# An encoder block on one core: the next head's convolution is issued inside the present head, the norms' products apart from their sums, and the first half's final norm between the second half's products

## The chip, the cores and the metric

The kernel runs on one core of a Trainium2 chip. A core has five engines with one instruction stream each: TensorE (PE, matrix products; its weight loads are listed as PEld and run beside the products), VectorE (DVE), ScalarE (ACT), GpSimd (POOL, hardly used here) and SyncE (SP), whose stream issues the DMA transfers. Each engine works through its own stream in order, and semaphores hold an instruction until what it reads is there and what it writes over has been read. The metric is device time in microseconds (us): median of three runs.

## What is computed

The reference, cut to what matters (D_MODEL = SEQ = 1024, hidden width 2816, four LRU heads of 256 channels):

```
u = rms_norm(x, g_mix);  u_a, x_b, gate_b, merge_a, merge_b = split(u @ w_in)
g_a      = gelu(u_a * s5_d + S5(u_a, forward) + S5(u_a, backward))
branch_a = (g_a * sigmoid(g_a @ s5_glu_w + s5_glu_b)) @ w_a_out
xc  = depthwise_conv4(x_b) + bias                       # RG-LRU, head by head
per direction d: r, i = sigmoid(xc @ wa + ba), sigmoid(xc @ wx + bx)
                 a = exp(-8 r softplus(-a_logit))
                 h_b += linear_scan(a, sqrt(1 - a*a) * (i * xc), reverse = d)
branch_b = (h_b * gelu(gate_b)) @ w_b_out
h = x + (sigmoid(merge_a)*branch_a + sigmoid(merge_b)*branch_b) @ w_o
v = rms_norm(h, g_ffn)
h = h + (silu(v @ w_ff_gate) * (v @ w_ff_up)) @ w_ff_down
h = h + sigmoid(rms_norm(h, g_ple) @ w_ple_gate) * (p @ w_ple_proj)
return rms_norm(h, g_final)
```

## The kernel before, in words

Activations lie feature by feature: a tile holds 128 features on the partitions and 1024 positions (or a half of 512). Every fp32 operand of a product is split into a high part and a rest (names that end in `h` and `l`); `gemm` forms three products per block of 128 by 128: high by high, rest by high, high by rest. A 128x512 product is one matmul, so a block of 1024 features against one tile of outputs is 24 products per half.

The order of work is that of the code, changed by a scheduler that builds each engine's stream. `hp()` raises a piece's priority; a tile waits for a free buffer of its pool. The pools that matter here: `l`, 16 tiles of 1024 for the LRU (`lslot`); `o`, 3 staging tiles (`ot`); two PSUM buffers `pg` for the gate products; from the Wo stage on, 8 PSUM banks.

The stages by the time at which they lie in the profiled execution: 0 to 505 us first norm, the projections u, x, g and the S5 branch; 505 to 698 the last projections (`pi_b`, `pi_a`), among whose products the LRU heads stand; 698 to 820 the S5 gate (`pgl`); 820 to 936 the product with w_a_out (`pao`); 936 to 1030 that with w_b_out (`pbo`); 1030 to 1136 w_o, half by half (`pwo`, with `pxr`, the transposes of x); 1136 to 1187 the first products of five hidden tiles (`head_group`: `q1`, `q2`) and the embedding's projection (`embed_proj`: `ppj`); 1187 to 1586 the hidden groups (`hidden_group`: up to seven products `q1` to `q7` of half size each); 1586 to 1835 the down projection (`pfd`), whose last block goes half by half; 1835 to the end the embedding's gate (`ppg`), half by half, and after each half the final norm (`pq`, sums; `pfin`, transposes back).

An LRU head (`lru_head`) begins with its convolution (`lru_conv`: per feature tile one ACT Identity at L718, three DVE operations at L719 to L721, the cast `xch` at L723 and the rest `xcl` at L724). Then per direction four gate products `pg` (24 products each on the operands `xch`, `xcl`; sigmoid to `tg`, tanh to `ls`) and the chain on DVE and ACT to the scan (L755 to L776). The heads are a generator of 16 steps, which `lru_step(share)` moves on between projections: `lru_step((i + 1) / NF)` after the i-th.

A norm (`rstd_parts`) sums squares (`pss`, products of one column, L942), works out the reciprocal root on DVE and ACT into a diagonal `dg`, and spreads it over the partitions by a product `psr` (L952). For the first half of w_o and both halves of the down projection the two products are issued one after the other (`rstd_half`).

A hidden group loads two weight tiles (L1045: `fg` for the gate, `fu` for up, into an `o` buffer) and makes sums and differences of them (`s1` to `s4`), the operands of `q3` to `q7`. A head group's result goes to DRAM as `hdd`, an `embed_proj` result as `prd`, both from `o` buffers.

Of the kernel before, what the change touches and what calls it, by code (L numbers as in the profile page):

```python
# [8 lines left out]
F32 = mybir.dt.float32  # L9
# [14 lines left out]
FILL = (1, 1, 1, 2)  # L24
PORD = "xgba"
NL = 16
LRUT = 6
MI = 2
WS, WH = 2, 3
XB = 2  # L30
# [4 lines left out]
D = 1024  # L35
# [18 lines left out]
def block_kernel(tc, a, out):  # L54
# [653 lines left out]
    def lru_conv(hd):  # L708
# [18 lines left out]
            xcl.append(cl)  # L727
        return xc, xch, xcl

    def lru_head(hd):  # L730
        xc, xch, xcl = lru_conv(hd)
        hf = [None, None]
        for d in range(2):
            with hp():
                st = wstage([128, 2, 2, 256], "l")
                for q, nm in enumerate(("lru_wa", "lru_wx")):
                    dma(st[:, q], a[nm][0, d, hd].rearrange("(k p) n -> p k n", p=128))
                wh, wl = split(st, [128, 2, 2, 256], "l")
            cc = [d * 8 + 2 * hd + m for m in range(2)]
            tr, ti, s, z = [], [], [], []  # L740
            for m in range(2):
                for bn, dst, q in (("lru_ba", tr, 0), ("lru_bx", ti, 1)):
                    ps = psb("pg")
                    gemm(ps, (wh[:, q], wl[:, q]), xch, xcl, ms=slice(m * 128, (m + 1) * 128))
                    t = lslot("tg")
                    A.activation(t, ps, AF.Sigmoid, bias=vcol(bn, cc[m]))
                    dst.append(t)

                s.append(lslot("ls"))
                A.activation(s[m], tr[m], AF.Tanh, scale=sp4[:, cc[m]:cc[m] + 1])  # L750
                V.tensor_tensor(ti[m], ti[m], xc[m], MUL)
                if m == 0:
                    yield
            for m in range(2):
                A.activation(tr[m], tr[m], AF.Exp, scale=spm8[:, cc[m]:cc[m] + 1])  # L755
                A.activation(tr[m], tr[m], AF.Identity, bias=ones[:, 0:1])

                z.append(lslot("lz"))
                V.scalar_tensor_tensor(z[m], s[m], 1.0, tr[m], ADD, MUL)
                V.scalar_tensor_tensor(z[m], z[m], 4.0, tr[m], SUB, MUL)  # L760
                V.tensor_scalar(tr[m], z[m], -0.5, -1.0, MUL, ADD)
                V.scalar_tensor_tensor(ti[m], z[m], -1.0, ti[m], MUL, MUL)
            for m in range(2):
                A.activation(s[m], s[m], AF.Sqrt, scale=0.25)
            for m in range(2):
                V.tensor_tensor(ti[m], ti[m], s[m], MUL)
                f = 2 * hd + m
                if d == 0:
                    V.tensor_tensor_scan(z[m], tr[m], ti[m], 0.0, MUL, ADD)
                    hf[m] = z[m]  # L770
                else:
                    V.tensor_tensor_scan(z[m][:, ::-1], tr[m][:, ::-1], ti[m][:, ::-1], 0.0, MUL, ADD)  # L772
                    V.tensor_tensor(hf[m], hf[m], z[m], ADD)
                    gg = lslot("gg")
                    dma(gg, ggd[f])
                    V.tensor_tensor(gg.rearrange("p (j c) -> p j c", j=8), hf[m].rearrange("p (c j) -> p j c", j=8),  # L776
                                    gg.rearrange("p (j c) -> p j c", j=8), MUL)
                    dma(ybd[f], gg)
            yield
# [52 lines left out]

    left = list(left)
    gp = []
    NF = len(left) + 8 + LRUT
    for i, kf in enumerate(left):
        inproj(*kf)
        if len(left) - i <= 4:
            gp.append(load_split(gd, len(gp), "ga", 1.0, y2))
        lru_step((i + 1) / NF)  # L840


    yad = [dram(f"yad{f}", [128, 1024]) for f in range(8)]
# [4 lines left out]
    for m in range(8):  # L848
        w = wload(a["s5_glu_w"][0][:, m * 128:(m + 1) * 128], f"gl{m}")
        ps = psm("pgl")  # L850
        gemm(ps, w, [x[0] for x in gp], [x[1] for x in gp])
        with hp():
            t = ot("glt")
            A.activation(t, ps, AF.Sigmoid, bias=vcol("s5_glu_b", m))
            g = ot("glg")
            dma(g, gd[m])
            V.tensor_tensor(t, t, g, MUL)
            dma(yad[m], t)
        if 1 <= m <= 4:
            yp.append(load_split(yad, m - 1, "ya", 1.0, r1))  # L860
        lru_step((len(left) + m + 1) / NF)
    while len(yp) < 8:
        yp.append(load_split(yad, len(yp), "ya", 1.0, y2))
    bp = []
    for m in range(8):
        w = wload(a["w_a_out"][0][:, m * 128:(m + 1) * 128], f"ao{m}")
        ps = psm("pao")
        gemm(ps, w, [x[0] for x in yp], [x[1] for x in yp])
        with hp():
            t = ot("ta")  # L870
            dma(t, mad[m])
            V.tensor_tensor(t, t, ps, MUL)
            dma(brd[m], t)
        lru_step((len(left) + 8 + m + 1) / NF)
        if m >= 4:
            bp.append(load_split(ybd, m - 4, "yb", 1.0, r1))
    while len(bp) < 8:
# [60 lines left out]
    def rstd_parts(n, acc):  # L938
# [13 lines left out]
        T.matmul(ps, ones, dg, start=True, stop=True)  # L952
        A.copy(rstd[:, half(n)], ps)
        yield

    def rstd_half(n, acc):
        for _ in rstd_parts(n, acc):
            pass

    def sumsq(h, first, acc):  # L960
        if first:
# [145 lines left out]
    def hidden_group(ht):  # L1107
# [3 lines left out]
        with hp(HPW):  # L1111
            w1 = raw_w(wg[:, cs], f"fg{ht}", "ws")
            w2 = raw_w(wu[:, cs], f"fu{ht}", "o")
            o = group_ops(w1, w2, f"_{ht}", head)
            ru = r1("ru", F32)
            if head:
                dma(ru, hdd[ht])
        p1, c11 = ru[:, 0:512], ru[:, 512:1024]
        if not head:
            q1 = bank("q1")  # L1120
# [61 lines left out]
    for n in range(2):  # L1182
        acc = qp.tile([128, 512], F32, name="acc", tag="acc", bufs=2)
        for m in range(8):
# [12 lines left out]
            V.tensor_tensor(h, h, ps, ADD)  # L1197
            dma(hsd[m][:, half(n)], h)
            sumsq(h, m == 0, acc)
            if n == 1 and m in (3, 5):  # L1200
                embed((m - 3) // 2)
            if n == 1 and m < 4:
                operands_first(m)
        if n == 0:
            rstd_half(n, acc)

# [15 lines left out]
    next(bcast)  # L1224
    fill(it, 0)
    fill(embed_proj(0), 0)
    next(bcast)
    fill(embed_proj(1), 1)
    pp = iter(range(2, 8))
    for ht in range(1, NHEAD):  # L1230
        it = head_group(ht)
        next(it)
        fill(it, FH)
        for m in [next(pp, None) for _ in range(2)]:
            if m is not None:
                fill(embed_proj(m), FP)
    for it in late:
        next(it)
    for _ in rest:
        pass  # L1240
    for ht in range(NHID):
        hidden_group(ht)


    hres = [r1(f"h{m}", F32) for m in range(8)]
# [24 lines left out]
    for k in range(8):  # L1270
        t = r1(f"uh{k}")
        uh.append([t[:, half(n)] for n in range(2)])
        ul.append([None, None])
    accs = []
    for n in range(2):
        acc = qp.tile([128, 512], F32, name="acc", tag="acc", bufs=2)
        accs.append(acc)
        cs = slice(n * 512, n * 512 + 512)
        for m2 in range(4):
            w = wload(wd[(h0 - nb) * 128:h0 * 128, m2 * 256:(m2 + 1) * 256], f"fe{n}_{m2}")  # L1280
            for mm in range(2):
                m = m2 * 2 + mm
                ps = bank("pfd")
                gemm([ps], w, fh, fl, ns=(n,), pn=0, ms=slice(mm * 128, (mm + 1) * 128))
                V.tensor_tensor(hres[m][:, cs], hres[m][:, cs], ps, ADD)
                ul[m][n] = act(f"ul{m}{n}", F32R)
                gain(m, n, "g_ple", uh, ul, acc)
            if n == 1 and m2 == 1:
                rstd_half(0, accs[0])
    for n in range(2):  # L1290
        cs = half(n)
        acc = qp.tile([128, 512], F32, name="acc", tag="acc", bufs=2)
# [1 line left out]
        for m in range(8):  # L1294
# [3 lines left out]
                dma(prj, prd[m][:, cs])  # L1298
            ps = bank("ppg")
            gemm([ps], w, uh, ul, ns=(n,), pn=0)  # L1300
            if n == 0 and m == 0:
                rstd_half(1, accs[1])
            t = qp.tile([128, 512], F32, name="vt2", tag="vt", bufs=4)
            V.tensor_tensor(t, rstd[:, cs], ps, MUL)
            A.activation(t, t, AF.Tanh, scale=0.5)
# [11 lines left out]
            elif m < 7:  # L1317
                V.tensor_tensor(acc, acc, q, ADD)
            V.tensor_scalar(hres[m][:, cs], hres[m][:, cs], vcol("g_final", m), None, MUL)

        pq = bank("pq"), bank("pq")
        sq = qp.tile([128, 12], F32, name="nsq", tag="nsq", bufs=2)
        for i, v in enumerate((acc, q)):
            for j in range(4):
                T.matmul(pq[i][:, j:j + 1], v[:, j * 128:(j + 1) * 128], ones[:, 0:1], start=True, stop=True)
        V.tensor_copy(sq[:, 0:4], pq[0][:, 0:4])
        V.tensor_tensor(sq[:, 0:4], sq[:, 0:4], pq[1][:, 0:4], ADD)
        A.activation(sq[:, 4:8], sq[:, 0:4], AF.Sqrt, bias=epsc, scale=1.0 / D)
        rstd_newton(sq[:, 4:8], sq[:, 0:4], sq[:, 8:12])
        for j in range(4):  # L1330
            ps = [bank("pfin"), bank("pfin")]
            for k in range(8):
                T.transpose(ps[k // 4][:, k % 4 * 128:(k % 4 + 1) * 128], hres[k][:, cs][:, j * 128:(j + 1) * 128], ident)  # L1333
            for e in range(2):
                o = act("fo")
                if e:
                    A.mul(o, ps[e], sq[:, 4 + j:5 + j])
                else:
                    V.tensor_scalar(o, ps[e], sq[:, 4 + j:5 + j], None, MUL)
                dma(oap[n * 4 + j][:, half(e)], o)  # L1340
    ctx.close()


# [22 lines left out]
```

## Time and profile before

| what | value |
|---|---|
| runs | 1956.99, 1952.87, 1952.08 us (median 1952.87) |
| profiled execution | 1958.97 us, of which the span 1957.1 |
| TensorE's mean granted clock | 0.979 of full |
| TensorE busy | 1866.2 us, 95% of the span |
| VectorE, ScalarE busy | 1319.2 us (67%), 907.2 us (46%) |
| transfers | 263.47 MB, mean 135 GB/s |

The busy time of an engine is the sum of its instructions. A window gives the busy time in a stretch of the span with the count of instructions in brackets, and the clock that TensorE was granted there, 1.00 being 2.4 GHz and 0.50 being 1.2 GHz. The chain is the sequence of instructions, transfers and waits that ended last, followed back from the end. A list of waits says which engine stood still at which line, and whose instruction at which line released it.

### The profile page before, as it was taken

The page shows a single profiled execution, that of the slowest core. Times are in us where ns is not written, and L with a number is a line of the kernel's source. Part 1 is how long each engine was busy: PE and PEld are TensorE (multiplying, and loading weights), DVE is VectorE, ACT ScalarE, POOL GpSimd, SP SyncE. Part 2 cuts the span into 40 slices and gives each one's busy share as a digit, 9 for nine tenths or more (in the row PEclk, how much of TensorE's full clock was granted, in tenths as well). Part 3 has the DMA queues.
Part 4 walks back from the last instruction along what each step waited for, and adds up shares of the span by engine and source line. Part 5 has one row for each costly group of instructions (what it writes and reads, how often), then busy time and mean ns, then how long its engine had stood idle before and what let it go on. Part 6 is the DMA issues. An engine that isn't in the chain of part 4 may idle for free.

```text
span 1957.1 us, 23256 instructions
## 1 busy us (share of the span) xinstructions
PE 1866.2 (95%) x8997; PEld 1549.8 (79%) x8997; DVE 1319.2 (67%) x1810; ACT 907.2 (46%) x1235; POOL 7.9 (0%) x60
## 2 busy tenths in 40 slices
PE   7999989899999999999999899999999999999898
PEld 6787777777787887778788787888888888888677
DVE  7517999998556667967544676877777774335666
ACT  5675666666465756675223453222323242113443
POOL 0000000000000000000000000000000000000000
PEclk8999999999999999999999999999999999999899
DMA  4794334443324364565545555423222283122342
GB/s 143 198 235 141 115 118 126 125 124 105 109 85 140 108 201 165 179 197 172 194 156 171 154 176 173 151 65 97 75 87 85 74 279 116 49 86 76 108 136 90
DMA packets 285854, 263.47 MB, mean 135 GB/s; under 512 B 32688, under 2 KB 244784, under 8 KB 285744
## 3 DMA queue, kind: packets, MB, share of 16 engines
q1 hardware_dynamic: 285744, 261.99, 43.0%
q8 instruction: 70, 1.15, 0.3%
q14 instruction: 40, 0.33, 0.1%
HBM read 185.86 MB, written 76.09 MB: 134 GB/s over the span
## 4 chain that ended last, share of the span: by engine, by line
PE 62%; DVE 5%; DMA 2%; ACT 2%; issue 2%; SPq 0%; ACTq 0%; DVEq 0%
PE q L1058 21%; PE pfd L159 12%; PE ppg L159 5%; PE pwo L159 4%; PE pg L159 4%; PE pbo L159 4%; PE pi_a L159 3%; PE pao L159 2%; PE pi_b L159 2%; PE pgl L159 2%; PE ppj L159 1%; DMA ld_yb<-ybd 1%; PE pfin L1333 1%; DMA xb<-xbd 1%; DVE lz L772 0%
## 5 line engine op out<-in xcount | busy, mean ns | idle before, releaser
L1265 DVE TENSOR_TENSOR h<-h,pfd 128x512 f32<-128x512 f32 x48 | 32.5, 683 | 114.0 <-PE pfd L159 114.0
L980 ACT CAST s<-rs 128x512 fp32r<-128x512 f32 x44 | 27.2, 618 | 150.4 <-DVE rs L1070 150.4
L159 PE MATMUL pfd<-fl,wh_fd 128*128 128x512 f32 x288 | 88.7, 389 | 0.0
L159 PE MATMUL pfd<-fh,wl_fd 128*128 128x512 f32 x288 | 88.7, 389 | 0.0
L159 PE MATMUL pfd<-fh,wh_fd 128*128 128x512 f32 x288 | 88.6, 389 | 0.0
L134 ACT CAST wh_fd<-ws_fd 128x768 fp32r<-128x768 f32 x24 | 20.1, 836 | 122.5 <-PE pfd L159 122.1
L159 PEld LDWEIGHTS pfd<-fh,wl_fd 128*128 128x128 f32 x288 | 54.1, 188 | 11.3
L1058 PE MATMUL q<-xt2h,s 128*128 128x512 f32 x176 | 59.5, 400 | 3.7 <-ACT s L980 3.7
L159 PEld LDWEIGHTS pfd<-fl,wh_fd 128*128 128x128 f32 x288 | 54.1, 188 | 11.2
L159 PEld LDWEIGHTS pfd<-fh,wh_fd 128*128 128x128 f32 x288 | 54.1, 188 | 11.2
L1058 PE MATMUL q<-xt3h,s 128*128 128x512 f32 x176 | 58.0, 390 | 0.0
L1058 PE MATMUL q<-xt1h,s 128*128 128x512 f32 x176 | 58.0, 390 | 0.0
L1058 PE MATMUL q<-xb1h,s 128*128 128x512 f32 x176 | 57.7, 389 | 0.0
L1058 PE MATMUL q<-xt4h,a 128*128 128x512 f32 x176 | 57.7, 389 | 0.0
L551 PE MATMUL pS<-U,mi 128*128 128x128 f32 x256 | 34.2, 290 | 22.6 <-ACT mi L538 22.6
L551 PEld LDWEIGHTS pS<-U,mi 128*128 128x128 f32 x256 | 31.2, 200 | 28.9 <-ACT mi L538 28.6
L159 PE MATMUL pg<-xch,wh_l 128*128 128x512 f32 x128 | 41.8, 419 | 11.3 <-ACT xch L723 11.3
L159 PE MATMUL pwo<-mh,wh_wo 128*128 128x512 f32 x128 | 51.8, 404 | 0.0
L159 PE MATMUL ppg<-uh,wh_pg 128*128 128x512 f32 x128 | 51.0, 398 | 0.0
L159 PE MATMUL ppg<-ul,wh_pg 128*128 128x512 f32 x128 | 50.5, 395 | 0.0
L159 PE MATMUL ppg<-uh,wl_pg 128*128 128x512 f32 x128 | 50.3, 393 | 0.0
L159 PE MATMUL pwo<-mh,wl_wo 128*128 128x512 f32 x128 | 50.1, 392 | 0.0
(544 smaller groups left out, 5405.9 us busy)
## 6 DMA issues: line engine op xcount, KB each, us to landing
ws_fg<-in_w_ff_gate_dram SPq DMA_DIRECT2D x22, 512.0 KB, 4.4
fu<-in_w_ff_up_dram SPq DMA_DIRECT2D x22, 512.0 KB, 4.0
hid<-up SPq DMA_DIRECT2D x22, 512.0 KB, 3.5
hid<-hid SPq DMA_DIRECT2D x22, 512.0 KB, 4.7
ws_fd<-in_w_ff_down_dram SPq DMA_DIRECT2D x24, 384.0 KB, 3.4
ws_wo<-in_w_o_dram SPq DMA_DIRECT2D x16, 512.0 KB, 4.0
ws_pg<-in_w_ple_gate_dram SPq DMA_DIRECT2D x16, 512.0 KB, 3.9
tb<-tab SPq DMA_DIRECT2D x16, 384.0 KB, 3.1
```

The costliest lines, as they stand in the source:

```text
L134: A.copy(wh, st)
L159: T.matmul(pn_[:, sub], ww[:, k0 + k, ms], xn[:, sub], start=(first and i == 0), stop=(last and i == tot - 1))
L551: T.matmul(pS[:, q * 128:(q + 1) * 128], mi[:, q, :], rhs, start=True, stop=True)
L980: A.copy(h, raw)
L1058: T.matmul(ps, ww[:, k], xx, start=i == 0, stop=i == 11)
L1265: V.tensor_tensor(hres[m][:, half(n)], hres[m][:, half(n)], ps[n], ADD)
L1333: T.transpose(ps[k // 4][:, k % 4 * 128:(k % 4 + 1) * 128], hres[k][:, cs][:, j * 128:(j + 1) * 128], ident)
```

## The change

Four things are done, all of them in the order in which work is issued.

First, the convolution of head hd+1 is issued inside head hd, after the gate products of its second direction and ahead of that direction's chain to the scan; that of head 0 stands ahead of the loop. The steps of the heads are spread over one slot fewer (`LRUT` 6 to 5, `len(left) + 8` to `+ 7`) and counted from i instead of i + 1.

Second, the two products of each norm are issued apart. For the first half of w_o the second one comes after the second half's products have begun, for the others after one or two further tiles; `operands_first` and `embed` move by a tile.

Third, the head groups and embedding projections are issued in another order (heads 1 and 2, `ppj` of tiles 2 and 3, heads 3 and 4, `ppj` of 4 to 7), and `hidden_group` is a generator, whose first part, the loads and operands, is issued for group 0 ahead of the `ppj` of tile 6.

Fourth, the final norm of the first half is issued in pieces between the second half's gate products.

```
-LRUT = 6
+LRUT = 5
...
+    convs = {}
     def lru_head(hd):
-        xc, xch, xcl = lru_conv(hd)
+        xc, xch, xcl = convs.pop(hd)
...
+            if d == 1 and hd < 3:
+                convs[hd + 1] = lru_conv(hd + 1)
             for m in range(2):
                 A.activation(tr[m], tr[m], AF.Exp, scale=spm8[:, cc[m]:cc[m] + 1])
...
-    NF = len(left) + 8 + LRUT
+    NF = len(left) + 7 + LRUT
+    convs[0] = lru_conv(0)
...
-        lru_step((i + 1) / NF)
+        lru_step(i / NF)
-        lru_step((len(left) + m + 1) / NF)
+        lru_step((len(left) + m) / NF)
-        lru_step((len(left) + 8 + m + 1) / NF)
+        lru_step((len(left) + 8 + m) / NF)
...
-            if n == 1 and m in (3, 5):
-                embed((m - 3) // 2)
-            if n == 1 and m < 4:
-                operands_first(m)
-        if n == 0:
-            rstd_half(n, acc)
+            if n == 1 and m < 2:
+                next(bcast)
+            if n == 1 and m in (4, 6):
+                embed((m - 4) // 2)
+            if n == 1 and 1 <= m < 5:
+                operands_first(m - 1)
+        bcast = rstd_parts(n, acc)
...
     fill(embed_proj(0), 0)
+    fill(embed_proj(1), 0)
     next(bcast)
-    fill(embed_proj(1), 1)
-    pp = iter(range(2, 8))
-    for ht in range(1, NHEAD):
+    groups = [hidden_group(ht) for ht in range(NHID)]
+    for ht, ms in ((1, ()), (2, (2, 3)), (3, ()), (4, (4, 5, 6, 7))):
         it = head_group(ht)
         next(it)
         fill(it, FH)
-        for m in [next(pp, None) for _ in range(2)]:
-            if m is not None:
-                fill(embed_proj(m), FP)
+        for m in ms:
+            if m == 6:
+                next(groups[0])
+            fill(embed_proj(m), FP)
...
-            if n == 1 and m2 == 1:
-                rstd_half(0, accs[0])
+            if n == 1 and m2 in (0, 2):
+                next(bcast[0])
+        bcast.append(rstd_parts(n, acc))
+    def final(n, acc, q):
...
-            if n == 0 and m == 0:
-                rstd_half(1, accs[1])
+            if n == 0 and m in (0, 2):
+                next(bcast[1])
+            if n == 1 and m in (1, 2, 3, 4, 5):
+                next(tail)
...
+        tail = final(n, acc, q)
+    for _ in tail:
+        pass
```

`final` holds the lines of the final norm as they were, with a `yield` after the sums and one after each quarter of the transposes.

How the streams change is shown at three places. VectorE between head 0 and head 1, before: `lz`, `tg`, `gg` belong to head 0's backward direction (scan at L772, sum at L773, product at L776), `xc`, `xcl` to head 1's convolution of its first feature tile, `wl_in_a` to the weights of a projection.

```order
L772 SCALAR_TENSOR_TENSOR lz<-tg 128x1024
L719 SCALAR_TENSOR_TENSOR xc<-xb,vec,xc 128x1022
L773 TENSOR_TENSOR lz<-lz 128x1024
L720 SCALAR_TENSOR_TENSOR xc<-xb,vec,xc 128x1023
L135 TENSOR_TENSOR wl_in_a_5189<-ws_in_a_5186,wh_in_a_5188 128x1024
L776 TENSOR_TENSOR gg<-lz,gg 128x1024
L721 SCALAR_TENSOR_TENSOR xc<-xb,vec,xc 128x1023
L724 TENSOR_TENSOR xcl<-xc,xch 128x1024
```

The same place after (the lines of the chain to the scan are five higher there: L764 for L759, L777 for L772).

```order
L753 TENSOR_TENSOR tg<-tg,xc 128x1024
L719 SCALAR_TENSOR_TENSOR xc<-xb,vec,xc 128x1022
L720 SCALAR_TENSOR_TENSOR xc<-xb,vec,xc 128x1023
L721 SCALAR_TENSOR_TENSOR xc<-xb,vec,xc 128x1023
L724 TENSOR_TENSOR xcl<-xc,xch 128x1024
L135 TENSOR_TENSOR wl_in_a_5189<-ws_in_a_5186,wh_in_a_5188 128x1024
L719 SCALAR_TENSOR_TENSOR xc<-xb,vec,xc 128x1022
L720 SCALAR_TENSOR_TENSOR xc<-xb,vec,xc 128x1023
L721 SCALAR_TENSOR_TENSOR xc<-xb,vec,xc 128x1023
L724 TENSOR_TENSOR xcl<-xc,xch 128x1024
L764 SCALAR_TENSOR_TENSOR lz<-ls,tg 128x1024 x2
```

Both feature tiles of head 1's convolution now stand ahead of head 0's last chain, where the first one stood behind its scan.

TensorE at the norm of the second half ahead of the embedding's gate, before: `ppg` is the gate's product, `wh_pg_13676` the first tile's weights, `wh_pg_13740` the second's.

```order
L159 MATMUL ppg<-ul_13462,wh_pg_13676 128x512
L159 MATMUL ppg<-uh_13284,wl_pg_13677 128x512
L942 MATMUL pss<-ones,acc 128x1 x4
L952 MATMUL psr<-dg,ones 128x512
L159 MATMUL ppg<-uh_13277,wh_pg_13740 128x512
```

The same place after.

```order
L159 MATMUL ppg<-ul_13462,wh_pg_13676 128x512
L159 MATMUL ppg<-uh_13284,wl_pg_13677 128x512
L948 MATMUL pss<-ones,acc 128x1 x4
L159 MATMUL ppg<-uh_13277,wh_pg_13737 128x512
L159 MATMUL ppg<-ul_13306,wh_pg_13737 128x512
```

The product `psr` has gone from here: it stands at 5243, with 48 products of two tiles between.

SyncE ahead of hidden group 0, before: `hdd` are the stores of head groups, `prd` those of the embedding's projection, `fu0` and `fu1` the loads of groups 0 and 1, `ru` the load of a head group's result.

```order
L1104 DMA hdd2_7734<-hd_8869 128x1024
L1104 DMA hdd3_7735<-hd_8967 128x1024
L1179 DMA prd6_7743<-prj_8988 128x1024
L1179 DMA prd7_7744<-prj_9026 128x1024
L1045 DMA fu0_9039<-in_w_ff_up_dram 128x8x128
L1045 DMA fu1_9143<-in_w_ff_up_dram 128x8x128
```

The same place after.

```order
L1106 DMA hdd3_7735<-hd_8945 128x1024
L1106 DMA hdd4_7736<-hd_8972 128x1024
L1182 DMA prd4_7741<-prj_8993 128x1024
L1047 DMA fu0_8999<-in_w_ff_up_dram 128x8x128
L1182 DMA prd5_7742<-prj_9037 128x1024
L1182 DMA prd6_7743<-prj_9055 128x1024
```

The load `fu0` stood behind the store of the last projected tile; it now stands behind that of tile 4, with three more to come.

## Rows read from the trace of the kernel before

**Rows 1.** The page, busy time of each engine: us, share of span, instructions
```profile
PE 1866.2 (95%) x8997; PEld 1549.8 (79%) x8997; DVE 1319.2 (67%) x1810; ACT 907.2 (46%) x1235; POOL 7.9 (0%) x60
```
**Rows 2.** Waits of TensorE: engine, line <- releaser: us total, times, longest
```profile
PE psr L952 <- DVE dg L949: 11.7, 3, 5.8
PE pg L159 <- ACT xch L723: 11.3, 4, 3.9
...
PE q L1058 <- ACT s L980: 3.7, 1, 3.7
PE py L626 <- DVE X L614: 3.5, 2, 2.0
PE pq L1325 <- ACT sqf L1314: 3.4, 1, 3.4
...
PE pbo L159 <- ACT ybh L821: 2.6, 1, 2.6
```
**Rows 3.** The chain of waits: start, us, what (two pieces)
```profile
1183.75 4.52 DMA fu<-in_w_ff_up_dram
...
1585.76 223.05 PE pfd L159 x984
```
**Rows 4.** Windows: stretch, its us, busy us (count) by engine, granted clock, DMA share
```profile
500.00:510.00 10.00, 7.96 (x40) 6.48 (x39) 6.33 (x6) 2.09 (x2) 0.00 (x0) 1.00 0.13 37
620.00:650.00 30.00, 26.31 (x103) 20.79 (x103) 18.61 (x15) 10.22 (x10) 0.00 (x0) 0.89 0.42 140
735.00:765.00 30.00, 26.52 (x104) 21.15 (x103) 21.16 (x17) 14.61 (x14) 0.00 (x0) 0.89 0.61 205
825.00:860.00 35.00, 31.06 (x125) 24.90 (x124) 23.60 (x20) 15.57 (x15) 0.00 (x0) 0.90 0.71 239
925.00:965.00 40.00, 36.86 (x149) 29.58 (x148) 24.45 (x21) 9.90 (x11) 0.00 (x0) 0.91 0.67 222
1075.00:1095.00 20.00, 14.60 (x62) 11.21 (x61) 12.13 (x25) 7.56 (x12) 0.00 (x0) 0.83 0.29 83
1180.00:1200.00 20.00, 16.31 (x59) 12.88 (x58) 10.34 (x17) 7.13 (x13) 0.00 (x0) 0.83 0.80 255
1810.00:1850.00 40.00, 30.77 (x124) 24.29 (x123) 25.36 (x53) 18.56 (x27) 0.00 (x0) 0.87 0.39 119
1880.00:1900.00 20.00, 16.55 (x84) 15.10 (x84) 12.23 (x23) 8.56 (x12) 0.00 (x0) 0.83 0.46 134
```
**Rows 5.** Timeline of TensorE, two kinds of transposes
```profile
1029.97 0.60 PE L1192 MATMUL pxr<-ident,xr 128*128 128x128 f32 x4
...
1891.17 6.41 PE L1333 MATMUL pfin<-ident,h 128*128 128x128 f32 x32
```
**Rows 6.** Timeline of VectorE from head 0's last gate product to head 1's operands
```profile
601.62 1.22 DVE L751 TENSOR_TENSOR tg<-tg,xc 128x1024 f32<-128x1024 f32 x1
...
622.35 1.25 DVE L719 SCALAR_TENSOR_TENSOR xc<-xb,vec,xc 128x1022 f32<-128x1022 f32 x1
...
628.91 1.27 DVE L721 SCALAR_TENSOR_TENSOR xc<-xb,vec,xc 128x1023 f32<-128x1023 f32 x1
631.35 1.23 DVE L724 TENSOR_TENSOR xcl<-xc,xch 128x1024 fp32r<-128x1024 f32 x1 [1.17 <-ACT xch L723]
```
**Rows 7.** Timeline of ScalarE at the same place
```profile
601.35 1.15 ACT L750 ACTIVATE ls<-tg,lt 128x1024 f32<-128x1024 f32 x1
602.51 1.28 ACT L755 ACT_TABLE_LOAD   x1
603.81 1.15 ACT L755 ACTIVATE tg<-tg,lt 128x1024 f32<-128x1024 f32 x1
...
614.00 1.23 ACT L718 ACTIVATE xc<-xb,vec 128x1024 f32<-128x1024 f32 x1
...
630.27 1.04 ACT L723 CAST xch<-xc 128x1024 fp32r<-128x1024 f32 x1 [7.15 <-DVE xc L721]
```
**Rows 8.** Window of the head groups and the embedding's projection
```profile
1136.00:1187.00 51.00, 51.00 (x228) 41.63 (x226) 41.54 (x74) 32.78 (x58) 0.00 (x0) 1.00 0.55 188
```

More of the change, by code (lines that the diff above doesn't have):

```diff
@@ L954, in rstd_parts @@
         yield
-    def rstd_half(n, acc):
-        for _ in rstd_parts(n, acc):
-            pass
     def sumsq(h, first, acc):
@@ L1117, in hidden_group @@
                 dma(ru, hdd[ht])
+        yield
         p1, c11 = ru[:, 0:512], ru[:, 512:1024]
@@ L1240, in block_kernel @@
         pass
-    for ht in range(NHID):
-        hidden_group(ht)
+    for g in groups:
+        for _ in g:
+            pass
     hres = [r1(f"h{m}", F32) for m in range(8)]
@@ L1273, in block_kernel @@
         ul.append([None, None])
-    accs = []
+    bcast = []
     for n in range(2):
         acc = qp.tile([128, 512], F32, name="acc", tag="acc", bufs=2)
-        accs.append(acc)
         cs = slice(n * 512, n * 512 + 512)
@@ L1287, in block_kernel @@
                 gain(m, n, "g_ple", uh, ul, acc)
-            if n == 1 and m2 == 1:
-                rstd_half(0, accs[0])
+            if n == 1 and m2 in (0, 2):
+                next(bcast[0])
+        bcast.append(rstd_parts(n, acc))
+    def final(n, acc, q):
+        cs = half(n)
+        pq = bank("pq"), bank("pq")
+        sq = qp.tile([128, 12], F32, name="nsq", tag="nsq", bufs=2)
+        for i, v in enumerate((acc, q)):
+            for j in range(4):
+                T.matmul(pq[i][:, j:j + 1], v[:, j * 128:(j + 1) * 128], ones[:, 0:1], start=True, stop=True)
+        V.tensor_copy(sq[:, 0:4], pq[0][:, 0:4])
+        V.tensor_tensor(sq[:, 0:4], sq[:, 0:4], pq[1][:, 0:4], ADD)
+        A.activation(sq[:, 4:8], sq[:, 0:4], AF.Sqrt, bias=epsc, scale=1.0 / D)
+        rstd_newton(sq[:, 4:8], sq[:, 0:4], sq[:, 8:12])
+        yield
+        for j in range(4):
+            ps = [bank("pfin"), bank("pfin")]
+            for k in range(8):
+                T.transpose(ps[k // 4][:, k % 4 * 128:(k % 4 + 1) * 128], hres[k][:, cs][:, j * 128:(j + 1) * 128], ident)
+            for e in range(2):
+                o = act("fo")
+                if e:
+                    A.mul(o, ps[e], sq[:, 4 + j:5 + j])
+                else:
+                    V.tensor_scalar(o, ps[e], sq[:, 4 + j:5 + j], None, MUL)
+                dma(oap[n * 4 + j][:, half(e)], o)
+            yield
     for n in range(2):
@@ L1319, in block_kernel @@
             V.tensor_scalar(hres[m][:, cs], hres[m][:, cs], vcol("g_final", m), None, MUL)
[L1321 to L1340, printed above, removed]
+        tail = final(n, acc, q)
+    for _ in tail:
+        pass
     ctx.close()
```

## The prediction
> **What bounds the kernel now.** The page's busy times come first: TensorE 95% of the span, VectorE 67%, ScalarE 46% [rows 1]. No edit here takes a product away, so all that can be won is time in which TensorE stands still or runs slowly. Second, the list of its waits gives the places: norms (`psr`, 11.7 us in three waits), the gate products waiting for the next head's cast (`pg` <- `xch`, 11.3 us in four), the first hidden group (3.7), the final norm's second sum (3.4), the first `pbo` product (2.6) [rows 2]. The waits before 505 us, the time at which the order begins to differ, I leave out. Third, the windows show that a wait costs more than itself. A window of 10 us with the S5 branch's wait of up to 2.0 us (`py`) kept the clock at 1.00; every window with a longer wait shows 0.83 to 0.91 [rows 2, 4]. So TensorE, after standing for 2.6 us or more, works for a while at the lower of its two levels, and I count both losses together: a stretch less its products at full speed. Full speed is 223.05 / 984 = 0.2267 us a product [rows 3].
>
> The places, by the windows in their order [rows 4]:
> - A, the handovers to heads 1, 2 and 3: 30 - 103 x 0.2267 = 6.65, 30 - 104 x 0.2267 = 6.42, 35 - 125 x 0.2267 = 6.66; together 19.7.
> - B, the first `pbo` product: 40 - 149 x 0.2267 = 6.2.
> - C, the norm of w_o's first half: of 62, 44 are products (9.97) and 18 small ones, to which I give 2.6 us (four `pxr` took 0.60 [rows 5]): 7.4.
> - D, hidden group 0: 20 - 59 x 0.2267 = 6.6.
> - E, the two norms ahead of the embedding's gate: of 124, 104 are products (23.58); the 20 small ones get 3.7: 12.7.
> - F, the first half's final norm: of 84, 36 are products (8.16); the 32 `pfin` took 6.41 [rows 5], half of that at the full level, and the 16 `pq` get 1.6: 20 - 8.16 - 3.2 - 1.6 = 7.0.
>
> Sum 59.6 us. This is all that the change can win.
>
> **The change, part by part.** Work is not added: the instructions are the same but for three more table loads on ScalarE, 3 x 1.28 us [rows 7] on an engine that is busy for 46% [rows 1]; where they delay an operand is counted below.
>
> *The convolution (A).* Before, the first tile's three DVE operations of head 1 stood among head 0's last chain, so that they began at 622.35, 20.7 us after the first DVE work behind the gate products (601.62), and TensorE, which had two projections (96 products, 21.8 us) to fill with, came to the gate products too early [rows 6]. Now they stand ahead of that chain. I count from T, the end of a head's last gate product. ScalarE does sigmoid (about 1.15 as its kind), tanh 1.15, table load 1.28, Exp 1.15, then the Identity 1.23 [rows 7]: 5.9. VectorE's three operations 3.8, ScalarE's cast 1.04, VectorE's rest 1.23 [rows 6, 7]: first tile ready at about 12. The second tile's Identity stands on ScalarE behind the sigmoid of the projection that ends at 10.9, and is done at about 15.4; then 3.8 + 1.04 + 1.23: 21.5. TensorE's order asks for it at about 23.2 (21.8 and 6 gate products). Head 1 is clear by 1.7, about 0.5 of its 6.65 staying where a weight tile's rest waits behind the longer chain: 6 won.
>
> At head 2 the second tile's cast stands behind a sigmoid of the S5 gate, which waits for TensorE at 21.8, and behind a load's cast; with both its rest comes at about 30, where TensorE asks for it between 29.7 and 31. Slack nothing, give or take 1: I take 5 of 6.4.
>
> At head 3 the convolution is done in time (21.5 as at head 1), but a new wait follows. The chain to head 2's scan now begins 2 x (3.8 + 1.23) = 10 us of DVE work later; it took 27.3 us before from its first to the next head's last operation (601.62 to 628.91 [rows 6]), half a tile's convolution, 3.8, within. T + 1.7 + 27.3 - 3.8 + 10, with five or six other DVE operations of 1.2 between (the S5 gate's): T + 41 to 42. Head 3's first sigmoid writes to a buffer of the 16 that this scan still reads, and the PSUM buffer which that sigmoid empties is wanted by the third gate product group some 175 products after T, at T + 39.6. TensorE waits about 2.5; behind the sigmoid on ScalarE stand another sigmoid, tanh and the cast of the next weights, which TensorE needs in turn. By the windows such a wait costs the clock too, as at `pbo` (2.6 waited, 6.2 lost), so I take 2 won of 6.66. The two loads of x_b that move with each convolution go to SyncE's queue behind a projection's store and weights and ahead of `gg` and of the store of the head's result, 20 us before the operands are due: I take them at nothing, and 5 us (a 512 KB load took 4.52 [rows 3]) late once if the queue holds them. Bounds for A: nothing (all three waits come back at the buffers) to 19.7; taken 6 + 5 + 2 = 13.
>
> The trace has the table load at 1.28 and the next activation 1.30 us after the load's start (602.51, 603.81) [rows 7]. The Trainium skill, ScalarE: Activation LUTs, "What ACT_TABLE_LOAD costs", gives a load of about 1.28 us and a drain of about 1.38 beside it, 2.66 for every switch. By the page each Identity behind a load would come 1.4 us later, the second handover would lose its slack, and the sum would be about 3 us poorer; by the trace, which shows no drain, it is as below, and the trace decides.
>
> *The step moved by a slot (B).* The last step of head 3 is now issued one `pao` tile earlier, 48 products, 10.9 us. The wait at `pbo` was 2.6 [rows 2], with more slack than it needs: 6 of 6.2, bounds 0 and 6.2.
>
> *The norms apart (C, E).* The chain from sums to diagonal held TensorE up to 5.8 us [rows 2]. Now 24 products (5.4 us) lie between `pss` and `psr` in C, 48 (10.9 us) at both places of E. In C `pss` is issued a tile later too, so that its operand is ready; 7 of 7.4. In E one `pss` has only about 1 us of margin: 12.3 of 12.7. Bounds for each: nothing, if VectorE's queue puts the diagonal behind the residual adds, to all. The two gate tiles between hold their PSUM banks until `rstd` is there; of eight banks five remain.
>
> *Group 0's load (D).* TensorE asked for the operand `s` when it was not there: the load `fu` was issued at 1183.75 and took 4.52 [rows 3], standing in SyncE's queue behind the store of the last `ppj` tile. Now three stores fewer stand ahead of it, that is 3 x 24 products = 16 us less. Against that VectorE: it was busy for 41.54 of 51 us in 74 instructions [rows 8], and gets group 0's nine operations of about 41.54 / 74 = 0.56 us, 5 us, into the same stretch. With 46.5 of 51 full, in order, and the `o` buffer of the load freed only by a head group's store, I put the operands some 2.3 us late instead of 3.7. A wait of 2.0 left the clock at 1.00 [rows 2, 4], so the 2.3 should cost little beside themselves. Bounds 0 and 6.6; taken 4.
>
> *The final norm (F).* `pq` comes after the second tile of the second half's gate products and each quarter of `pfin` after another tile; 5.4 us of products cover each, where the wait was 3.4 [rows 2]. The stores of the output go with them, between SyncE's loads of the second half's weights and `prd` tiles; only the last weight tile stands behind one of them. 6.7 of 7.0, bounds 0 and 7.0. The end of the kernel, behind the last product, is as before.
>
> **Sum.** 13 + 6 + 7 + 4 + 12.3 + 6.7 = 49 us. Against the profiled execution (1958.97; span 1957.1) that is 1910; that execution lies 6.1 us above the median of the runs, 1952.87, from which the same 49 us leave 1904.
>
> **The rivals.**
> - *The handovers come back.* The waits for `xch` go, and TensorE stands as long at the gate's PSUM buffers, since the chains and scans that free the `l` tiles start 10 us later. For it: the count at head 3 (41 to 42 against 39.6). Against: the same count gives buffers free at T + 36 for 38 at head 1 and at T + 44 for 46 at head 2. A gives nothing: 49 - 13 = 36, 1917 us.
> - *Group 0 keeps its wait*, so that the early issue does not do what it says: the stores ahead of `fu` and the full VectorE queue set its time as before. D gives nothing: 45, 1908 us.
> - *All clear.* Every place of the list loses nothing: 1952.87 - 59.6 = 1893 us.
> - *Slower: the scans starve the heads.* Two convolutions ahead of each chain hold their three tiles per feature tile longer (6 of the 16 `l` buffers), and each head's gate products stand until the whole backward chain of the head ahead is through. If that comes one further stretch of 27.3 us of DVE work later [rows 6], TensorE, which has 96 products between, stands for some 20 us and then runs 3 slowly: 23 for 6.6 at each of three handovers, 3 x 16.4 = 49 more, against 36 won at B to F: 1952.87 - 36 + 49 = 1966 us. It decides from 36 / 3 + 6.6 = 18.6 lost at each handover. Against it: the buffers freed by the forward chain suffice for the next head's first gate group in my count.
>
> **How the numbers follow.** What a measurement of this kernel can tell from no change is about 0.3%, 5.9 us: 1947.0 to 1958.7. Forecast 50%, its own range 1898 to 1911 (head 2 and head 3 each 3 us either way, D 2 to 4 either way); handovers come back 21%; all clear 11%; group 0 keeps its wait 8%; scans starve the heads 4%; something unseen 6%, of it half within 0.3% (new waits that eat what the old ones gave), two sixths faster, one sixth slower. Faster 50 + 21 + 11 + 8 + 2 = 92%, same 3%, slower 5%. The range runs from below all clear (1893, with 3 us for small waits that I did not count) to past the handovers' return with D at nothing (1917 + 4 = 1921, and 5 for one further new wait): 1890 to 1926.
>
> **What would show it.** Right: in windows with 103 products the clock at 1.00 and no `pg` <- `xch` wait of over 2 us at heads 1 and 2; one wait of about 2.5 at head 3, released by a sigmoid or a scan and not by a cast; no wait at `pbo`, `psr` and `pq`; `q` <- `s` at about 2; `pfin` 3.2 instead of 6.4. Wrong: `pg` waits whose sum is still over 11 us, a `psr` wait released by `dg`, or a new wait elsewhere (the first half's `pwo`, the `ppj` tiles, or `ppg` waiting for a bank) with a clock below 0.95 in its window.

## The result and the profile after

The changed kernel takes 1909.99 us (median of four runs, 1907.41 to 1910.35) where the kernel before took 1953.67 in the same session (four runs, 1952.08 to 1956.99): a ratio of 0.9766, 95% interval 0.9754 to 0.9779. A second comparison gave 1908.51 against 1954.95, 0.9764 (0.9750 to 0.9777). The forecast was 1904, with a range of 1890 to 1926: right in direction and, but for one place, in mechanism, and 6 us too low. The profiled execution after took 1907.41.

The busy times of the page after, to be held against [rows 1]:

```profile
PE 1841.4 (97%) x8997; PEld 1532.0 (80%) x8997; DVE 1315.1 (69%) x1810; ACT 909.7 (48%) x1238; POOL 7.8 (0%) x60
```

The work is the same, down to the number of instructions on TensorE; it is busy for 25 us less because it ran at the lower clock less often (mean granted clock 0.994, before 0.979). TensorE's waits after, from 500 us on (as [rows 2]: us in total, times, longest):

```profile
PE q L1060 <- ACT s L982: 3.9, 1, 3.9
PE pg L159 <- ACT tg L748: 3.2, 1, 3.2
PE pq L1303 <- ACT sqf L1346: 3.0, 1, 3.0
...
PE pbo L159 <- DVE ybl L827: 0.5, 1, 0.5
...
PE pbo L159 <- ACT ybh L826: 0.2, 1, 0.2
```

The waits for `dg`, for the convolution's cast `xch` and for the middle `pq` are gone; the `pq` that is left is the one at the very end, which no product can cover. Two waits stand out: hidden group 0 (`q` <- `s`), as long as before, and a new one at a gate product, released by a sigmoid (`tg`). The same places as in [rows 4], by the products they hold:

```profile
500.00:510.00 10.00, 7.97 (x47) 6.71 (x46) 5.15 (x4) 2.09 (x2) 0.00 (x0) 1.00 0.00 0
615.00:645.00 30.00, 30.00 (x134) 24.84 (x133) 25.23 (x21) 14.36 (x15) 0.00 (x0) 1.00 0.26 89
735.00:765.00 30.00, 30.00 (x134) 24.85 (x133) 29.14 (x24) 26.98 (x25) 0.00 (x0) 1.00 0.70 218
805.00:840.00 35.00, 31.85 (x134) 25.84 (x132) 34.96 (x29) 25.41 (x24) 0.00 (x0) 0.95 0.72 240
905.00:945.00 40.00, 39.32 (x172) 31.95 (x172) 21.14 (x19) 10.45 (x11) 0.00 (x0) 1.00 0.74 234
1055.00:1075.00 20.00, 20.00 (x99) 16.39 (x98) 13.41 (x27) 9.22 (x15) 0.00 (x0) 1.00 0.58 172
1150.00:1170.00 20.00, 15.72 (x62) 12.27 (x61) 11.54 (x19) 9.11 (x17) 0.00 (x0) 0.91 0.95 301
1775.00:1815.00 40.00, 40.00 (x182) 32.65 (x181) 32.03 (x63) 23.03 (x33) 0.00 (x0) 1.00 0.52 165
1850.00:1870.00 20.00, 20.00 (x105) 16.96 (x104) 14.70 (x29) 11.15 (x15) 0.00 (x0) 1.00 0.49 156
```

In six of the eight lines after the first, TensorE's busy time is the stretch, or within 1 us of it, and the clock is 1.00. Heads 1 and 2 are clear. Head 3 loses 35 - 134 x 0.2267 = 4.6, `pbo` 40 - 172 x 0.2267 = 1.0, group 0 20 - 62 x 0.2267 = 5.9. Together 11.5 us are lost where 59.6 were.

Head 3 is as the prediction counted it. TensorE and ScalarE there:

```profile
825.56 0.73 PE L159 MATMUL pg<-xch,wh_l 128*128 128x512 f32 x2 [3.15 <-ACT tg L748]
```

```profile
823.09 1.28 ACT L748 ACT_TABLE_LOAD   x1 [4.87 <-DVE lz L777]
824.39 2.12 ACT L748 ACTIVATE tg<-pg,vec 128x1024 f32<-128x1024 f32 x2
```

ScalarE stood 4.87 us for head 2's scan before it could load the table for head 3's sigmoid, and TensorE 3.15 for that sigmoid (some 2.5 expected).

Group 0 is not as counted. SyncE, VectorE and TensorE ahead of its first product:

```profile
1149.08 1.53 SPq L1106 DMA_DIRECT2D hdd<-hd  x2
1150.70 0.41 SPq L1182 DMA_DIRECT2D prd<-prj  x1
1151.77 0.38 SPq L1047 DMA_DIRECT2D fu<-in_w_ff_up_dram  x1
```

```profile
1155.15 0.69 DVE L983 TENSOR_TENSOR xb1l<-hp,xb1h 128x512 fp32r<-128x512 f32 x1 [3.08 <-PE ppj L159]
1156.15 0.69 DVE L983 TENSOR_TENSOR xb1l<-hp,xb1h 128x512 fp32r<-128x512 f32 x1 [0.31 <-ACT xb1h L982]
1157.16 0.69 DVE L983 TENSOR_TENSOR xb1l<-hp,xb1h 128x512 fp32r<-128x512 f32 x1 [0.31 <-ACT xb1h L982]
1157.77 0.68 DVE L1071 TENSOR_TENSOR rs<-fu 128x512 f32<-128x512 f32 x1
```

```profile
1160.36 0.50 PE L1060 MATMUL q<-xt2h,s 128*128 128x512 f32 x1 [3.86 <-ACT s L982]
```

The load `fu` is issued 4.7 us before TensorE asks for its sums (1160.36 - 3.86 = 1156.50), after two stores of head groups, whose values VectorE finished only at 1149.06 and 1150.26, and one of the projection. And the sum `rs` stands in VectorE's queue behind three rests of the operand `xb1`, which only the group's last product needs, and which wait for the last `ppj` products: VectorE stood idle for 3.08 us with `rs` behind, at first with the load still under way (the shares are worked out below, at D).

### The profile page after: what moved, and what is told of

Read it like the earlier page. It is cut to its first block, busy times and chain, and to the rows that moved or that the text cites. A ratio compares the mean times of both kernels' runs of the same rounds, so it can differ in the third digit from the quotient of the medians.

```text
span 1905.2 us, 23270 instructions
## 1 busy us (share of the span) xinstructions
PE 1841.4 (97%) x8997; PEld 1532.0 (80%) x8997; DVE 1315.1 (69%) x1810; ACT 909.7 (48%) x1238; POOL 7.8 (0%) x60
## 4 chain that ended last, share of the span: by engine, by line
PE 68%; DVE 2%; DMA 1%; ACT 1%; issue 1%; DVEq 0%; ACTq 0%
PE q L1060 22%; PE pfd L159 13%; PE pwo L159 5%; PE ppg L159 5%; PE pi_a L159 5%; PE pgl L159 5%; PE pg L159 4%; PE pbo L159 4%; PE pi_b L159 3%; PE pao L159 2%; PE ppj L159 1%; DMA ld_yb<-ybd 1%; DMA brd<-ta 1%; PE pfin L1312 0%; PE pxr L1195 0%
## 5 line engine op out<-in xcount | busy, mean ns | idle before, releaser
L134 ACT CAST wh_fd<-ws_fd 128x768 fp32r<-128x768 f32 x24 | 20.1, 835 | 122.1 <-PE pfd L159 121.4
L159 PEld LDWEIGHTS pfd<-fh,wh_fd 128*128 128x128 f32 x288 | 54.1, 188 | 11.2
L159 PEld LDWEIGHTS pfd<-fh,wl_fd 128*128 128x128 f32 x288 | 54.1, 188 | 11.2
L159 PE MATMUL pwo<-ml,wh_wo 128*128 128x512 f32 x128 | 49.8, 389 | 0.0
```

The source lines that it names most:

```text
L134: A.copy(wh, st)
L159: T.matmul(pn_[:, sub], ww[:, k0 + k, ms], xn[:, sub], start=(first and i == 0), stop=(last and i == tot - 1))
```

## The experiments

**The four parts apart.** Each is the kernel before with one part of the diff. The convolution with the shift of the steps, b_conv:

```
+            if d == 1 and hd < 3:
+                convs[hd + 1] = lru_conv(hd + 1)
...
-        lru_step((i + 1) / NF)
+        lru_step(i / NF)
```

> The kernel before with the first part of the change alone: the next head's convolution inside the present head, and the steps of the heads shifted by a slot. Terms add up (theory): A and B go as in the changed kernel, whose windows lose 4.6 us at head 3 and 0.7 at pbo where the kernel before lost 19.7 and 6.2: 20.6 us faster, some 1933 us; the waits pg <- xch and pbo <- ybh are gone, psr and pq stay. Rival (the gain needs the other parts, or is given back at w_o): within 10 us of before.

1938.43 against 1954.64, 16.2 less (ratio 0.9916, 0.9904 to 0.9929): the theory in kind, short by 4 us. The `xch` waits are gone; the new wait at head 3 is there at 3.2 us, and `pbo` still waits for 1.6. Its windows lose 35 - 128 x 0.2267 = 6.0 us at head 3 (805 to 840) and 20 - 78 x 0.2267 = 2.3 at `pbo` (930 to 950), where the text had taken 4.6 and 0.7 (the changed kernel's idle time at `pbo`; by products it loses 1.0 there).

The norms, b_norms, and the final norm, b_tail:

```
-            if n == 1 and m2 == 1:
-                rstd_half(0, accs[0])
+            if n == 1 and m2 in (0, 2):
+                next(bcast[0])
```

```
+            if n == 1 and m in (1, 2, 3, 4, 5):
+                next(tail)
```

> The kernel before with the norms' products apart (w_o's first half, both halves ahead of the embedding's gate; operands_first and embed one tile later) and nothing else. Theory: C and E go, 7.4 + 12.7 = 20.1 us faster, some 1934 us, no psr wait left. Rival (the later operands of the head groups meet the unchanged head stage, which has VectorE at 41.5 of 51 us, and lose there what C wins): 12 to 13 us faster, with a wait at q1 or at hidden group 0 over 7 us.

> The kernel before with the first half's final norm between the second half's gate products and nothing else. Theory: F goes, 7 us faster, some 1947 us, no pq wait in the middle and 32 pfin products at the full clock. Rival (the extra work on VectorE and ScalarE between the gate tiles delays the last ones, and the end of the kernel is as much later): no change.

1932.87, 21.8 less (0.9890, 0.9875 to 0.9905), no `psr` wait: C and E are worth what was counted, and nothing is lost in the head stage, where `q` <- `s` stays at 3.6. b_tail 1949.12, 5.5 less (0.9970, 0.9958 to 0.9981): F, with 7.0 expected; the end of the kernel did not give it back.

The head stage, b_heads:

```
+    for ht, ms in ((1, ()), (2, (2, 3)), (3, ()), (4, (4, 5, 6, 7))):
...
+            if m == 6:
+                next(groups[0])
```

> The kernel before with the third part alone: head groups and the embedding's projection in the new order, the loads and operands of hidden group 0 issued ahead of the projection's tile 6. The changed kernel lost 5.95 us at group 0, before 6.6. Theory (the early issue does not do what it says): within 1.5 us of before, some 1953 us. Rival (it helps by the 4 us that were forecast, and something else in the changed kernel spoiled it): 1949 us, with a wait q <- s of under 2.5 us.

1955.37 against 1954.64, ratio 1.0007 (0.9997 to 1.0017). Alone, too, the early issue wins nothing; the wait stays, at 3.9 in the profile:

```profile
PE q L1058 <- ACT s L980: 3.9, 1, 3.9
```

The four add up: 16.2 + 21.8 + 5.5 - 0.7 = 42.8, where the whole change measured 43.7 and 46.4.

**The changed kernel again**, a_again, as the base of the next three.

> The changed kernel once more, as the base of the three runs beside it: 1907 to 1911 us, a wait of some 3.2 us at head 3 (pg <- tg) and of 3.9 at hidden group 0 (q <- s). If the first profile was typical, pbo waits for less than 1 us; if that wait changes from run to run, it is up to 2 here.

1908.51 (1907.57 to 1909.34), the same two waits at 3.2 and 3.9; at `pbo` only the 0.5 for `ybl`.

**Group 0: two ways to free its load.** a_fh2 issues fewer steps of operand work after each head group; a_vt stages the projection's results elsewhere than in the three `o` buffers:

```
-FH, FP = 4, 3
+FH, FP = 2, 3
```

```
-        t = ot("prj")
         for n in range(2):
-            A.copy(t[:, half(n)], ps[n])
-        dma(prd[m], t)
+            t = qp.tile([128, 512], F32, name="prj", tag="vt", bufs=4)
+            A.copy(t, ps[n])
+            dma(prd[m][:, half(n)], t)
```

> The changed kernel, with two and not four steps of operand work after each head group, so that VectorE's work is spread and the load of group 0 stands ahead of the stores of head 4 and of the projection's tile 4 in SyncE's queue. Theory (VectorE's backlog: the load was issued at 1151.77, behind the stores of heads 3 and 4, whose values VectorE finished 6 us after their last product): the load is issued before 1148, the wait q <- s falls from 3.9 to under 1.5, 4 to 6 us faster than the changed kernel beside it. Rival (the three staging buffers set the time): within 1.5 us of it.

> The changed kernel, with the results of the embedding's projection staged in the small tiles of 512 and not in the three staging buffers, which leaves these to the head groups and to the load of group 0. Rival (buffers): the load is issued several us earlier, the wait q <- s falls under 1.5 us, 4 to 6 us faster than the changed kernel beside it. Theory (VectorE's backlog): the wait stays over 2.5 us, less than 2 us faster, since the sums for s stand behind the same VectorE work.

1901.71 (1899.65 to 1904.08) and 1902.63 (1901.48 to 1905.23): 6.8 and 5.9 less than beside it, and neither profile has a `q` <- `s` wait left. Each theory held in the run made for it (in a_fh2 the load came at 1148.95, though, and not before 1148) and failed in the other's, so neither VectorE's backlog nor the buffers alone is the cause. What both have in common is the place of the load. In a_vt, SyncE and VectorE:

```profile
1145.35 0.38 SPq L1047 DMA_DIRECT2D fu<-in_w_ff_up_dram  x1
```

```profile
1149.52 0.69 DVE L1071 TENSOR_TENSOR rs<-fu 128x512 f32<-128x512 f32 x1 [0.66 <-DMA fu<-in_w_ff_up_dram]
```

In a_fh2:

```profile
1148.95 0.38 SPq L1047 DMA_DIRECT2D fu<-in_w_ff_up_dram  x1
```

```profile
1154.18 0.69 DVE L1071 TENSOR_TENSOR rs<-fu 128x512 f32<-128x512 f32 x1
1154.78 0.69 DVE L983 TENSOR_TENSOR xt4l<-hp,xt4h 128x512 fp32r<-128x512 f32 x1
1155.38 0.69 DVE L1072 TENSOR_TENSOR rs<-rs,ws_fg 128x512 f32<-128x512 f32 x1
```

TensorE's first product of group 0 starts at 1156.54 in a_vt and at 1158.97 in a_fh2, without a wait: the load is issued 11.2 and 10.0 us ahead of it, and the scheduler has put `rs` ahead of the `xb1l` rests, which begin at 1158.57 and 1160.20. Both runs change the load's time and VectorE's order together; no run changes one alone. In a_fh2's profile the clock also stayed up at head 3 (last section), so that not all of its 6.8 need be group 0's.

**Head 3: the buffers.** a_r1 gives the four sigmoids of head 3's forward gates tiles of another pool, a_r1b the two tanh as well:

```
-                    t = lslot("tg")
+                    t = r1("tg", F32) if hd == 3 and d == 0 else lslot("tg")
...
-                s.append(lslot("ls"))
+                s.append(r1("ls", F32) if hd == 3 and d == 0 else lslot("ls"))
```

> The changed kernel, with the four gate tiles of head 3's forward direction in the pool of long-lived tiles, which has free buffers there, and not in the pool of 16. Theory (the wait at head 3 is for a buffer that head 2's backward scan still reads): the wait of 3.2 us goes, and with it the 4.6 us lost there: 4 to 5 us faster than the changed kernel beside it. Rival (the scan is late on VectorE, and the gates wait for it in another way, at the next buffer or at head 3's own chain): less than 1.5 us faster, a wait of 2 us or more at pg or pao close by.

> The changed kernel, with all six tiles of head 3's forward gates (four sigmoids, two tanh) in the pool of long-lived tiles. With only the four sigmoids there, the wait at pg went and one of 5.4 us came at pao, since the tanh's tile, of the pool of 16, was free only after the same scan (ScalarE stood 4.55 us for lz) and held the weights' cast behind it. Theory (16 buffers are what head 3 waits for): no wait over 1.5 us at pg or pao, 4 to 5 us faster than the changed kernel's 1908.5 (1904). Rival (VectorE is behind there, and the product waits for the weights' rest or for gates whichever buffer is free): a wait of 2 us or more stays, within 1.5 us of 1908.5.

1911.81 and 1910.28, no faster than 1908.51. The wait at `pg` goes and another comes a little later. In a_r1 ScalarE waits at the next tile of the pool for the same scan, in front of the weights' cast:

```profile
825.64 1.15 ACT L752 ACTIVATE ls<-tg,lt 128x1024 f32<-128x1024 f32 x1 [4.55 <-DVE lz L777]
```

In a_r1b, with no such tile left, TensorE waits for the rest of the weights, which VectorE makes:

```profile
PE pao L159 <- DVE wl_ao L135: 4.7, 1, 4.7
```

The rival was right in kind (a_r1b is 1.8 us above 1908.5, where it had 1.5): buffers are what head 3 waits for first, and VectorE is what it waits for when it has them. The changed kernel's windows say so too; VectorE, the third busy time of a row, is busy for 10.00 of 10 us in both:

```profile
820.00:830.00 10.00, 6.85 (x24) 5.21 (x23) 10.00 (x7) 6.87 (x6) 0.00 (x0) 0.85 0.87 295
830.00:840.00 10.00, 10.00 (x45) 8.22 (x44) 10.00 (x9) 9.06 (x10) 0.00 (x0) 0.98 0.71 224
```

**Head 3: the spacing of the steps.** b_convonly is the kernel before with the convolution alone, `LRUT`, `NF` and `lru_step((i + 1) / NF)` left as they were:

```
+            if d == 1 and hd < 3:
+                convs[hd + 1] = lru_conv(hd + 1)
```

> The kernel before with the convolution moved and the steps of the heads where they were. With the steps shifted as well it took 1938.4 us, 16.2 less than before. Theory (the step shift is worth what stands at pbo, a wait of 1.0 to 2.6 us in the profiles so far, 3 us with the clock; the moved convolution brings the rest): 1941 us, 13 less than before, the pbo wait still over 1.5 us, head 3's wait for a buffer still there at some 3 us. Rival (the shift is what gives the convolution its room at the handovers): less than 8 us below before, with pg <- xch waits left.

1934.82 (0.9903, 0.9888 to 0.9917), 20.3 less than before and 3.6 less than b_conv by the medians, though the two intervals overlap. Its waits between 505 and 960 us:

```profile
PE pbo L159 <- ACT ybh L826: 1.3, 1, 1.3
PE pg L159 <- ACT tg L748: 0.5, 1, 0.5
PE pbo L159 <- DVE ybl L827: 0.5, 1, 0.5
PE pg L159 <- ACT xch L723: 0.3, 1, 0.3
```

Neither text expected this: at head 3 no wait is left. The `pg` <- `tg` of 0.5 stands at head 2, among the products of the S5 gate:

```profile
741.95 0.73 PE L159 MATMUL pg<-xch,wh_l 128*128 128x512 f32 x2 [0.54 <-ACT tg L748]
```

Between the first two gate groups of head 3 stand two blocks of `pao` products here (811.66 to 833.42, 21.8 us); with the shift it is one block and the first products of the next (810.46 to 822.40 in the changed kernel, 11.9 us). The shift brings the second group forward, onto the scan of head 2.

**Both losses away.** best1 is a_r1b with the edit of a_fh2; best2 is a_fh2 with the steps as in the kernel before:

```
-FH, FP = 4, 3
+FH, FP = 2, 3
-LRUT = 5
+LRUT = 6
...
-    NF = len(left) + 7 + LRUT
+    NF = len(left) + 8 + LRUT
-        lru_step(i / NF)
+        lru_step((i + 1) / NF)
```

> The changed kernel with both: six tiles of head 3 in the other pool, and two steps of operand work after each head group. If the two losses are apart, 6.8 and 4.5 us off 1908.5: some 1897 us. If the first does nothing (VectorE behind), 1901.7 as with the second alone.

> The changed kernel, with the steps of the heads where they were in the kernel before and two steps of operand work after each head group. The run with the convolution alone moved was 3.6 us faster than with the shift, since the shift leaves one product block of w_a_out (48 products) between the first two gate groups of head 3 and not two. Theory (that spacing makes the wait at head 3, and the step of operand work the one at group 0; both apart): no wait over 1 us at pg, pbo up to 1.8, 1901.7 - 3.6 = some 1898 us. Rival (the shift pays at pbo what it costs at head 3 once the rest is clear): 1901 to 1903 us.

best1 took 1904.85, more than either sum of its text, with the `pao` wait of 4.7 still there: the pool adds nothing. best2 took 1899.90 (1898.83 to 1904.37), ratio to before 0.9734 (0.9721 to 0.9747); a_fh2 has 0.9729 (0.9716 to 0.9743). The head 3 wait has gone from best2's profile, as the theory said (the 0.5 for `tg` is at head 2, at 741.30):

```profile
PE pbo L159 <- ACT ybh L826: 1.3, 1, 1.3
PE pbo L159 <- DVE ybl L827: 0.5, 1, 0.5
PE pg L159 <- ACT tg L748: 0.5, 1, 0.5
```

But the ratios can't be told apart, and `pbo` waits 1.3 + 0.5. Whether the step shift pays stays open. That a_fh2 and best2 are faster than the changed kernel is shown: their intervals end below its 0.9754 and 0.9750.

## Why the prediction was right, and the steps that were not

Its measure of what could be won held: lost time counted from products at 0.2267 us gave 59.6, of which 59.6 - 11.5 = 48.1 went by the windows, with 49 forecast. By term:

| place | forecast | windows, before less after | run of the part alone |
|---|---|---|---|
| A, handovers | 13 | 19.7 - 4.6 = 15.1 | 16.2 with the shift, 20.3 without (A and B) |
| B, `pbo` | 6 | 6.2 - 1.0 = 5.2 | |
| C, E, norms | 19.3 | 20.1 | 21.8 |
| D, group 0 | 4 | 6.6 - 5.9 = 0.7 | -0.7 |
| F, final norm | 6.7 | 7.0 | 5.5 |

*A.* The count from T was right at each head. The rest of the second tile, counted for T + 21.5, 30 and 21.5, is done at T + 22.2, 30.1 and 22.4 (heads 1 to 3). At head 3 the new wait came in kind and place, and 2.1 of 6.66 were won, 2 taken. Its size, 3.15 for 2.5, is partly luck: TensorE asked at T + 39.0 (39.6 counted) and head 2's scan let the buffer go at T + 39.6 (41 to 42 counted), which alone would have been 0.6; the table load and the sigmoid behind the scan, 823.09 to 825.56, were not counted and made 2.5. What it did not see is that head 3's wait belongs to the shift of the steps (b_conv against b_convonly), and that free buffers would not have helped (a_r1b).

*C, E, F.* Right in mechanism and size.

*D.* This step failed: "I put the operands some 2.3 us late instead of 3.7". It began with a wrong sum, "3 x 24 products = 16 us less" for the load. A `ppj` tile is 12 products:

```profile
1142.80 2.73 PE ppj L159 x12
```

Three tiles are 8.2 us, and the store of head group 4, which stood behind the load, now stands ahead of it. The load was issued 4.7 us before TensorE asked for `s`, where it had been 1190.89 - 3.7 - 1183.75 = 3.4: 1.3 us were won, not 16. The operands came 3.86 late, and 0.42 for the rest of `s` behind that. The rival with 8%, that group 0 keeps its wait, is what happened, at the 1908 us that it gave; it is the wait that shows it, since in the total the other misses happen to cancel. Of its two reasons, the stores ahead of `fu` are half of it; VectorE's queue, the other, was not full, but stood. A load takes some 4.2 us (a_vt: 1145.35 to `rs` at 1149.52), so that of the changed kernel was there at about 1155.9. In the kernel before, the chain from the load's end (1183.75 + 4.52 = 1188.27, [rows 3]) to the first product was 2.6 us:

```profile
1188.29 0.69 DVE rs L1069
...
1190.89 1.22 PE q L1058 x2
```

1155.9 + 2.6 is 1158.5, 2.0 after TensorE asked: nearly the 2.3, though not by its sum. The other 1.9 is `rs` behind `xb1l`, begun at 1157.77 and not at 1155.9. The prediction priced VectorE by how full its queue was and not by what stands in it ahead of `rs` and waits.

*B and the starting point.* The losses were counted in one execution, 1958.97, 5.3 us above the median of 1953.67, and part of that excess lay in a wait that was counted as won: `pbo` waited 2.6 for `ybh` there, but 1.0, 1.4 and 1.5 in the profiles of b_heads, b_norms and b_tail, which leave that place as it was. The profiled executions differ by 1958.97 - 1907.41 = 51.6 us, the medians by 43.7. B's term of 6 was mis-sized by this; by the window 940 to 960 that place lost 20 - 61 x 0.2267 = 6.2 in the execution counted, but 3.2 in b_norms and 3.7 in b_tail.

*The table load.* At head 3 it took 1.28 us, from 823.09, and the sigmoids behind it began at 824.39, 1.30 later, as in [rows 7]. The drain that the Trainium skill (ScalarE: Activation LUTs, "What ACT_TABLE_LOAD costs") adds shows in neither trace.

## What to carry to other kernels

Count what TensorE can win as stretch less products at full speed, not as idle time: here the waits of [rows 2] at the six places sum to 32.7 of the 59.6 us, and most of the rest is the clock (from its second line on, TensorE's busy times in [rows 4] are 23.7 us longer than their products at full speed; an estimate, since the small products go in at the prediction's figures). When a load is issued earlier in the code, look at what stands ahead of it in the DMA queue, and then at what stands ahead of its first reader in that engine's queue and waits for something else; free buffers, or less work ahead, move both. Take the size of a wait from more than one execution where the term is a few us.

## What was not expected of the hardware

The same wait did not always cost the clock. At head 3 TensorE stood some 3.1 us in a_fh2 as in the changed kernel, but kept 1.00 in a_fh2, here and in the next 10 us, and did 72 products from 820 to 840 instead of 69, though it stood 0.5 us more:

```profile
820.00:830.00 10.00, 6.85 (x30) 5.37 (x29) 10.00 (x9) 4.98 (x5) 0.00 (x0) 1.00 0.77 243
```

And at `pbo` a wait of 1.5 + 0.5 us in b_tail came with a lower clock, where 1.6 + 0.5 in b_conv kept 1.00 (930 to 950):

```profile
940.00:950.00 10.00, 7.94 (x28) 5.24 (x27) 5.59 (x5) 2.67 (x3) 0.00 (x0) 0.86 0.99 310
```

The 2.0 of `py` left it at 1.00 in [rows 4] and after, and up to 520 us in both; but in b_conv the 10 us behind the same wait show the lower clock:

```profile
510.00:520.00 10.00, 10.00 (x45) 8.65 (x44) 1.23 (x1) 3.84 (x4) 0.00 (x0) 0.83 0.42 133
```

So "2.6 us or more" in the prediction was no bound, and that 2.0 us cost no clock held in its one execution; what decides was not tried.
